# Two down projections of a decoder layer, from eight half-size block products to seven

## The chip, the cores and the metric

One core of a Trainium2 chip runs the whole program in one launch. The metric is the device time of one execution in microseconds (us); the value given is the median of three runs. The profile shows one execution, its times counted from the start of its span. In the text, PE is TensorE, DVE is VectorE, ACT is ScalarE, POOL is GpSimd and SP is the engine whose queue issues nearly all loads and stores; PSUM and SBUF are the two on-chip memories.

## The reference: what is computed

A decoder layer on 1024 tokens of width 1024: a feed-forward half step, a token mixer with two branches, and a second feed-forward half step. Cut to what matters here (the two half steps have their own weights and modulation vectors; `sh`, `sc`, `gt` are three of nine vectors that `silu(c) @ w_mod + b_mod` gives):

```python
def swiglu(h, w_gate, w_up, w_down):          # h [1024, 1024], w_gate, w_up [1024, 2816], w_down [2816, 1024]
    return (jax.nn.silu(h @ w_gate) * (h @ w_up)) @ w_down
h = rms_norm(x, g_pre_ffn1[l]) * (1 + sc1) + sh1
x = x + 0.5 * gt1 * rms_norm(swiglu(h, w_gate1[l], w_up1[l], w_down1[l]), g_post_ffn1[l])
u = rms_norm(x, g_pre_mix[l]) * (1 + sc2) + sh2
y = hybrid_mixer(u, positions, w_in[l], ...)
x = x + gt2 * rms_norm(y, g_post_mix[l])
```

All inputs and the output are fp32. The change concerns `@ w_down`, once in each half step.

## The kernel before

**Products.** Every matmul operand is a pair, hi (fp32r) and lo (the rest). `split` (L75 to L77) makes it: ACT copies the source to hi, DVE subtracts hi from the source to get lo; `psplit` (L79 to L82) has GpSimd subtract. A product is three matmuls, `mm3` (L102 to L106): hi·hi (L104), lo·hi (L105), hi·lo (L106).

**Stages.** They follow each other in the program: the first vectors of the modulation; FFN1's `gate_up`; FFN1's `down`; the mixer (`mixer_front`, `branch_b`, branch A, `mixer_out`); FFN2's `gate_up`; FFN2's `down`. All DMA loads and most stores are issued by SP, in the order of the program. The order on each engine is set by the framework's scheduler, which simulates a timeline of the program.

**gate_up** (L252 to L361) makes act = silu(h w_gate) * (h w_up), transposed, in DRAM (`actd`, 22 chunks of 128 rows by 1024 tokens). It works in 11 blocks of two chunks; each block is seven products (`i` 0 to 6) of half size, each with eight `mm3` chains into banks `gu`, 168 matmuls of 128x512 a block. GpSimd adds blocks of the raw weights `rw` (L286 to L289), `split` makes `wh` and `wl` of them three products ahead (LOOK), DVE adds the results to partial sums `p` (L343, L346), ACT takes the silu (L349), GpSimd multiplies (L351), and SP stores to `actd` (L353). In FFN1 the products 0 and 1 of the first five blocks (EARLY) come first, then products 2 to 6 of these blocks, then blocks 5 to 10 whole.

**The filler.** FFN1's `gate_up` runs a generator beside its products, `mod_rest` (L166 to L201): seven vectors of the modulation. One step (of 126) loads a [128, 512] tile `wr` of `w_mod` (four buffers, shared with a partial sum of the early blocks) and multiplies it into `macc` on DVE (L183, L185); after eight such steps `macc` is split (`mah`, `mal`), summed by PE (`mo`, L191, L192), and a row is finished on DVE (L194 to L199) and written to DRAM. Two steps (FILL) run after each product of blocks 5 to 10; the other 42 steps run in FFN1's `down`.

**down** (L368 to L425) computes G * (act w_down): three groups, columns 0 to 511 for all eight token tiles, then columns 512 to 1023 for token tiles 0 to 3, then for tiles 4 to 7. A group runs over all 22 chunks: one `mm3` per tile and chunk into bank `dn`, 1056 matmuls of 128x512 in all. The weights `rd` and the act tiles (kept in SBUF, `room`, made by `rooms`, L1158) are split for each group anew (`dh`, `dl`, `ah`, `al`). `evac` (L363 to L366) takes a bank: ACT squares it with a sum, DVE multiplies it by the gain. While the third group runs, the generator `post` works on tokens 0 to 511, one step per chunk, because their rows are complete: 

- FFN1: `post1` (L1234): `residual` (L1129, one 1024-wide DVE operation and eight or so 128x1 ones), `prenorm` (L1136, the same again), then `emit_hT` (L115), which transposes the four tiles on PE (L122) into `uh` and `ul` (L123, L124), the operand of `mixer_front`, whose first product is `cpj<-wc0h,uh`.
- FFN2: `post2` (L1337): residual and the store of the output, with the 128x1 operations on GpSimd except for the last tile.

## Time and profile before

| | us |
|---|---|
| runs | 2540.12, 2541.58, 2545.11 |
| median | 2541.58 |
| span of the profiled execution | 2537.8 |
| FFN1 gate_up: early products, blocks 0 to 4, blocks 5 to 10 | up to 119, to 263, to 498.8 |
| FFN1 down | 498.8 to 754.3 |
| mixer | 754.3 to about 2000 |
| FFN2 down, then what follows its last matmul | 2284.8 to 2525.7, to 2537.8 |
| PE busy | 2393.8 (94% of the span) |

The profiled execution is known by its span alone. The median of the runs stands 3.8 us above the span, the lowest run 2.3 us. Read it first by engine (who is busy for nearly the whole span), then by stage (the windows), then by the waits inside a stage: an engine that is idle for long in one stage may be the one that others wait for in another.

### The profile page before, as it was taken

What the parts mean: (1) busy time and instruction counts of PE and PEld (TensorE: products, weight loads), DVE (VectorE), ACT (ScalarE), POOL (GpSimd) and SP (SyncE); (2) the same over time, 40 slices, a digit from 0 to 9 for tenths busy, and PEclk for the clock granted to TensorE, in tenths of its full rate; (3) what the DMA queues carried; (4) which work ended last, traced back from release to release, by engine and by line L of the source; (5) the groups of instructions that cost most, each with busy time, mean ns of one, the idle gap of its engine ahead of it and who ended that gap; (6) DMA issues with size and microseconds to landing.
All of it is one profiled execution on the core that took longest, in us unless ns stands there. A gap on an engine that the chain in (4) does not pass through costs nothing.

```text
span 2537.8 us, 34341 instructions
## 1 busy us (share of the span) xinstructions
PE 2393.8 (94%) x11471; PEld 2017.5 (79%) x11471; DVE 1613.0 (64%) x3209; ACT 1096.6 (43%) x2358; POOL 953.3 (38%) x1109
## 2 busy tenths in 40 slices
...
GB/s 280 89 109 128 149 154 158 253 203 50 193 137 110 79 84 115 181 26 94 12 40 53 79 66 64 51 183 144 111 123 123 97 75 90 86 188 111 51 108 149
DMA packets 226222, 291.67 MB, mean 115 GB/s; under 512 B 23095, under 2 KB 145879, under 8 KB 226045
## 3 DMA queue, kind: packets, MB, share of 16 engines
...
q14 instruction: 87, 0.70, 0.1%
...
## 4 chain that ended last, share of the span: by engine, by line
PE 75%; DVE 11%; DMA 5%; issue 3%; POOL 3%; ACT 2%; SPq 0%; DVEq 0%; POOLq 0%; ACTq 0%
PE gu L105 8%; PE gu L104 8%; PE gu L106 8%; PE dn L105 6%; PE dn L106 6%; PE dn L104 6%; DMA wr<-in_w_mod_dram 3%; PE gpj L104 2%; PE gpj L105 2%; PE gpj L106 2%; PE bq L104 2%; PE bq L105 2%; PE bq L106 2%; PE bv L105 1%; PE bv L106 1%
## 5 line engine op out<-in xcount | busy, mean ns | idle before, releaser
L104 PE MATMUL gu<-V,wh 128*128 128x512 f32 x1232 | 489.6, 398 | 16.5 <-ACT wh L76 8.4
L105 PE MATMUL gu<-V,wl 128*128 128x512 f32 x1232 | 488.8, 397 | 6.8 <-DVE wl L77 6.1
L106 PE MATMUL gu<-V,wh 128*128 128x512 f32 x1232 | 483.4, 395 | 5.1 <-DVE V L77 5.1
L77 DVE TENSOR_TENSOR wl<-rw,wh 128x512 fp32r<-128x512 f32 x232 | 215.1, 930 | 136.3 <-PE gu L105 94.4
L104 PEld LDWEIGHTS gu<-V,wh 128*128 128x128 f32 x1232 | 235.7, 191 | 70.3 <-ACT wh L76 9.1
L105 PEld LDWEIGHTS gu<-V,wl 128*128 128x128 f32 x1232 | 235.3, 191 | 61.7 <-DVE wl L77 10.0
L106 PEld LDWEIGHTS gu<-V,wh 128*128 128x128 f32 x1232 | 234.0, 190 | 57.5 <-DVE V L77 7.9
L105 PE MATMUL dn<-dh,al 128*128 128x512 f32 x704 | 275.6, 392 | 1.5 <-DVE al L77 1.4
L106 PE MATMUL dn<-dl,ah 128*128 128x512 f32 x704 | 274.6, 391 | 0.0
L104 PE MATMUL dn<-dh,ah 128*128 128x512 f32 x704 | 253.7, 391 | 6.0 <-DVE junk L197 6.0
L76 ACT CAST wh<-rw 128x512 fp32r<-128x512 f32 x232 | 140.0, 618 | 208.3 <-PE gu L106 125.4
L351 POOL TENSOR_TENSOR p<-p 128x512 f32<-128x512 f32 x86 | 129.0, 1500 | 245.5 <-ACT wh L81 68.7
L343 DVE TENSOR_TENSOR p<-gu,p 128x512 f32<-128x512 f32 x252 | 170.2, 682 | 65.1 <-PE gu L106 35.1
L76 ACT CAST ah<-act 128x512 fp32r<-128x512 f32 x176 | 107.5, 621 | 182.6 <-PE dn L105 133.0
L77 DVE TENSOR_TENSOR al<-act,ah 128x512 fp32r<-128x512 f32 x176 | 118.2, 690 | 83.9 <-PE dn L105 40.8
L104 PEld LDWEIGHTS dn<-dh,ah 128*128 128x128 f32 x704 | 132.6, 189 | 33.9 <-DVE junk L197 6.4
L105 PEld LDWEIGHTS dn<-dh,al 128*128 128x128 f32 x704 | 132.8, 189 | 30.5 <-DVE al L77 3.0
L77 DVE TENSOR_TENSOR dl<-rd,dh 128x512 fp32r<-128x512 f32 x132 | 91.3, 692 | 102.1 <-PE dn L105 50.4
L106 PEld LDWEIGHTS dn<-dl,ah 128*128 128x128 f32 x704 | 132.9, 189 | 27.8
L349 ACT ACTIVATE p<-p 128x512 f32<-128x512 f32 x86 | 54.5, 633 | 215.6 <-DVE p L343 161.8
L185 DVE SCALAR_TENSOR_TENSOR macc<-wr,scol,macc 128x512 f32<-128x512 f32 x98 | 93.9, 958 | 52.2 <-DMA wr<-in_w_mod_dram 51.4
L76 ACT CAST dh<-rd 128x512 fp32r<-128x512 f32 x132 | 81.7, 619 | 84.9 <-PE dn L105 71.3
...
## 6 DMA issues: line engine op xcount, KB each, us to landing
...
```

The lines of the kernel that those rows point to most:

```text
L76: self.nc.scalar.copy(hi, src)
L77: self.nc.vector.tensor_sub(lo, src, f(hi))
L104: mm(out, ah, bh, start=start, stop=False)
L105: mm(out, al, bh, start=False, stop=False)
L106: mm(out, ah, bl, start=False, stop=stop)
L185: nc.vector.scalar_tensor_tensor(acc, r, self.scol[:, k:k + 1], acc, op0=ALU.mult, op1=ALU.add)
L343: nc.vector.tensor_tensor(x[m], bk, y[m], op=ALU.add)
L349: nc.scalar.activation(x[0], x[0], AF.Silu)
L351: nc.gpsimd.tensor_tensor(x[1], x[1], x[0], op=ALU.mult)
```

## The change

`down` becomes seven products of half size. With act^T split into four blocks (rows: halves of the 2816; columns: halves of the tokens) and w_down into four, P1 to P7 are 4 token tiles x 11 chunks x 3 matmuls each, 132, so 924 per FFN where there were 1056. Two sets of four banks take turns. The sums of act blocks are made in place by GpSimd (44 operations of 128x512 per FFN, in P2, P3 and P4); the four sums of w_down's blocks are made by the generator `mix_down`, GpSimd again, and go to a DRAM tensor `wx`: 22 tiles per FFN, each two loads of 256 KB, four subtractions of 128x256 and four stores of 128 KB, three steps a tile. For FFN1 they run as a filler in `gate_up`, one step after each product from product 2 of block 0 on, with two steps of `mod_rest` beside each (`both`); `mod_rest` now ends inside `gate_up`. For FFN2 they run in `branch_b`, five steps per token tile of its groups 1 and 2. The results are put together by `o1` to `o7`: DVE adds, ACT squares from SBUF, GpSimd multiplies by the gain in 12 of 16 cases. Tokens 0 to 511 are complete when P6 ends, so `post(0)` runs beside P7, and `post(1)` after it.

The diff, cut to its core:

```diff
-FILL = 2            # steps of the filler after each product or chunk
+FILL = 1
...
-                if filler is not None and b >= len(early):
+                if filler is not None:
...
+    def mix_down(self, pool, wd, out):
         nc = self.nc
...
+        NJ = DFF // P // 2
+        for j in range(NJ):
+            for q in range(2):
+                r = pool.tile([P, 2, 2, 256], F32, name="wx", bufs=1)
+                for e in range(2):
+                    nc.sync.dma_start(r[:, e], wd[0, (NJ * e + j) * P:(NJ * e + j + 1) * P, :]
+                                      .rearrange("p (c f) -> p c f", c=2)[:, :, q * 256:(q + 1) * 256])
+                yield
+                b11, b12, b21, b22 = (r[:, e, c] for e in range(2) for c in range(2))
+                sub = lambda o, x, y: nc.gpsimd.tensor_tensor(o, x, y, op=ALU.subtract)
+                sub(b11, b12, b11)
+                sub(b12, b22, b12)
+                sub(b22, b22, b11)
+                sub(b21, b22, b21)
+                yield
+                for n, t in enumerate((b11, b22, b12, b21)):
+                    nc.sync.dma_start(out[n, j * P:(j + 1) * P, q * 256:(q + 1) * 256], t)
+                yield
+    def down(self, W, W2, wd, wx, rooms, actd, y, G, junk, ss, post):
+        nc = self.nc
+        NJ = DFF // P // 2
+        tags = (("tr", "tr", "o", "gg"), ("pj", "pj", "s", "pt"))
+        a11, a12, a21, a22 = (rooms[n] for n in ("11", "12", "21", "22"))
+        src = lambda n, j: actd[j + NJ * (n[1] == "2"), :, 512 * (n[0] == "1"):512 * (n[0] == "1") + 512]
+        load = lambda n, j: nc.sync.dma_start(rooms[n][j], src(n, j))
+        add = lambda o, x, z, op: nc.gpsimd.tensor_tensor(o, x, z, op=op)
+        raw = lambda r, c: wd[0, r * NJ * P:(r + 1) * NJ * P, c * 512:(c + 1) * 512]
+        dsl = [slice(0, 512), slice(512, 1024)]
+        C = lambda r, c, t: y[2 - r][:, t, dsl[c - 1]]
+        sq = lambda r, c, t: ss[4 * (2 - r) + t][:, c - 1:c]
+        V = nc.vector.tensor_tensor
+        def normed(r, c, t, E):
+            nc.scalar.activation(junk(), C(r, c, t), AF.Square, accum_out=sq(r, c, t))
+            E.tensor_tensor(C(r, c, t), C(r, c, t), G[:, dsl[c - 1]], op=ALU.mult)
+        def o1(b, t):
+            nc.scalar.copy(C(2, 2, t), b)
+        def o4(b, t):
+            nc.scalar.copy(C(2, 1, t), b)
+        def o2(b, t):
+            V(C(1, 1, t), C(2, 2, t), b, op=ALU.add)
+            normed(1, 1, t, nc.gpsimd)
+        def o6(b, t):
+            V(C(1, 2, t), C(2, 2, t), b, op=ALU.add)
+            add(C(2, 1, t), C(1, 2, t), C(2, 1, t), ALU.subtract)
+        def o5(b, t):
+            V(C(1, 2, t), C(1, 2, t), b, op=ALU.add)
+        def o7(b, t):
+            for c in (1, 2):
+                V(C(2, c, t), C(2, 1, t) if c == 1 else C(1, 2, t), b, op=ALU.add)
+                normed(2, c, t, nc.gpsimd if c == 1 else nc.vector)
+        def o3(b, t):
+            V(C(1, 2, t), C(1, 2, t), b, op=ALU.add)
+            normed(1, 2, t, nc.gpsimd)
+        def s14(j):
+            load("12", j)
+            load("21", j)
+        def s1(j):
+            add(a22[j], a21[j], a22[j], ALU.add)
+        def s23(j):
+            add(a21[j], a11[j], a21[j], ALU.subtract)
+            add(a11[j], a22[j], a11[j], ALU.subtract)
+        none = lambda j: None
+        prods = [(None, raw(0, 0), 0, o1, lambda j: load("22", j), none),
+                 (a22, wx[3], 1, o4, s14, s1),
+                 (a12, raw(1, 0), 0, o2, lambda j: load("11", j), s23),
+                 (a11, wx[1], 1, o6, none, lambda j: add(a12[j], a12[j], a11[j], ALU.subtract)),
+                 (a22, wx[0], 0, o5, none, none),
+                 (a21, wx[2], 1, o7, none, none),
+                 (a12, raw(1, 1), 0, o3, none, none)]
         bg = iter(())
...
+        for n, (A, B, s, end, before, after) in enumerate(prods):
+            bk = [self.bank("dn", tag=x) for x in tags[s]]
+            final = n == len(prods) - 1
+            nlate = LATE + (W2 is not None) * 2 if final else 1
+            late = []
+            def mul(t, j, w, a):
+                ts = slice(t * P, (t + 1) * P)
+                self.mm3(bk[t], a[0][:, ts], a[1][:, ts], w[0], w[1], j == 0, j == NJ - 1)
+            for j in range(NJ):
+                before(j)
+                if j % 2 == 0:
+                    m = min(2, NJ - j)
                     r = self.raw([P, 2, 512], "rd")
...
+                    nc.sync.dma_start(r[:, 0:m], B[j * P:(j + m) * P, :].rearrange("(k p) f -> p k f", p=P))
+                    if A is None:
+                        ra = self.raw([P, 2, 512], "ra")
+                        nc.sync.dma_start(ra[:, 0:m], actd[j:j + m, :, 512:1024].rearrange("c p f -> p c f"))
+                pool = W2 if W2 is not None and final and NJ - nlate <= j < NJ - nlate + 2 else W
+                w = [pool.tile([P, 512], F32R, name=f"d{x}", tag="w") for x in "hl"]
+                self.split(w[0], w[1], r[:, j % 2])
+                a = [pool.tile([P, 512], F32R, name=f"a{x}", tag="w") for x in "hl"]
+                self.split(a[0], a[1], ra[:, j % 2] if A is None else A[j])
+                after(j)
+                if j >= NJ - nlate:
+                    late.append((j, w, a))
                     continue
...
+                for t in range(4):
+                    mul(t, j, w, a)
+                if final:
                     next(bg, None)
...
+                    next(bg, None)
             for _ in bg:
                 pass
...
+            for t in range(4):
                 for x in late:
                     mul(t, *x)
...
+                end(bk[t], t)
+            if end is o7:
+                bg = post(0)
+            if final:
+                bg = post(1)
         for _ in bg:
             pass
...
-    def branch_b(self, uT, W, bp, last, gates, raws):
+    def branch_b(self, uT, W, bp, last, gates, raws, mix):
...
+                mix = mix(self.rawp)
...
+                if g:
+                    for _ in range(5):
+                        next(mix, None)
...
+    def both(a, b):
+        while True:
+            done = True
+            for g, n in ((a, 2), (b, 1)):
+                for _ in range(n):
+                    for _ in g:
+                        done = False
+                        break
+            if done:
+                return
+            yield
...
     def rooms(fp):
-        """Room of [128, 512] for each chunk and half of the tokens: 16 of each half in big, the others in fp[half]."""
-        r = [L.big.tile([P, 8, 512], F32, name="act", tag="big") for _ in range(4)]
-        f2 = [[fp[h].tile([P, 512], F32, name=f"act{c}{h}") for h in range(2)] for c in range(16, DFF // P)]
-        return [[r[2 * h + c // 8][:, c % 8] for h in range(2)] for c in range(16)] + f2
-
-    # first half step
+        r = {}
+        for n in ("22", "21", "12", "11"):
+            t = L.big.tile([P, 8, 512], F32, name="act", tag="big")
+            r[n] = [t[:, c] for c in range(8)] + [fp[n[0] == "1"].tile([P, 512], F32, name=f"act{n}{c}") for c in range(3)]
+        return r
...
-            fill = L.mod_rest(wk, jkf)
+            wx1 = L.dram.tile([4, DFF // 2, 512], F32, name="wx1")
+            mix = L.mix_down(fs, aps["w_down1"], wx1)
+            fill = both(L.mod_rest(wk, jkf), mix)
             GU([(b, i) for b in range(EARLY) for i in range(2, 7)] + [(b, i) for b in range(EARLY, NB) for i in range(7)], fill)
+            for _ in fill:
+                pass
...
-            L.down(W, None, aps["w_down1"], room, actd, y, A1, lambda: jkb, ss, post1, fill)
-
...
+        wx2 = L.dram.tile([4, DFF // 2, 512], F32, name="wx2")
...
-            L.branch_b(uT, W, bp, lambda: L.topk(sc, ixp, mask, off, bp), lambda: L.gates(uT, gp), raws)
+            L.branch_b(uT, W, bp, lambda: L.topk(sc, ixp, mask, off, bp), lambda: L.gates(uT, gp), raws,
+                       lambda p: L.mix_down(p, aps["w_down2"], wx2))
...
-            L.down(W, W2, aps["w_down2"], room, actd, y, G3, lambda: jk, ss, post2)
+            L.down(W, W2, aps["w_down2"], wx2, room, actd, y, G3, lambda: jk, ss, post2)
```

The order of the instructions shows three places where the change moves work. The first is DVE in block 7 of FFN1's `gate_up`, from a `p_...` addition of one product to the first addition of the next (`macc` and `mal` are the filler's, `wl` the lo parts of weights, `junk` a finished row of the modulation). Before:

```order
L343 TENSOR_TENSOR p_2879<-gu,p_2879 128x512
L185 SCALAR_TENSOR_TENSOR macc<-wr,scol,macc 128x512
L77 TENSOR_TENSOR wl_3100<-rw_2815,wh_3099 128x512
L77 TENSOR_TENSOR mal<-macc,mah 128x512
L343 TENSOR_TENSOR p_2879<-gu,p_2879 128x512
L77 TENSOR_TENSOR wl_3109<-rw_2817,wh_3108 128x512
L77 TENSOR_TENSOR wl_3148<-rw_2815,wh_3147 128x512
L77 TENSOR_TENSOR wl_3152<-rw_2817,wh_3151 128x512
L343 TENSOR_TENSOR p_3172<-gu,p_3125 128x512
```

The same place with the change:

```order
L343 TENSOR_TENSOR p_3235<-gu,p_3235 128x512
L77 TENSOR_TENSOR wl_3482<-rw_3163,wh_3481 128x512
L183 TENSOR_SCALAR macc<-wr,scol 128x512
L185 SCALAR_TENSOR_TENSOR macc<-wr,scol,macc 128x512
L77 TENSOR_TENSOR wl_3525<-rw_3161,wh_3524 128x512
L185 SCALAR_TENSOR_TENSOR macc<-wr,scol,macc 128x512
L197 TENSOR_TENSOR junk_95<-mo,junk_95 1x512
L185 SCALAR_TENSOR_TENSOR macc<-wr,scol,macc 128x512 x2
L77 TENSOR_TENSOR wl_3529<-rw_3163,wh_3528 128x512
```

More of the filler stands between the same additions and splits: counted over blocks 5 to 9, 57 rows of `macc` become 95, 7 of `mal` become 12, and 14 short `junk` rows become 20, beside unchanged 70 additions and 60 `wl`.

The second place is PE at the end of FFN1's `down`, up to the first product of the mixer (`tr` are the transposes of tokens 0 to 511). Before:

```order
L104 MATMUL dn<-dh,ah 128x512
L105 MATMUL dn<-dh,al 128x512
L106 MATMUL dn<-dl,ah 128x512
L122 MATMUL tr_6202<-ident,y_4135 128x128 x4
L122 MATMUL tr_6229<-ident,y_4135 128x128 x4
L104 MATMUL cpj<-wc0h,uh_6032 128x384
```

With the change (seven more rows of `tr_6367` and `tr_6374` stand ahead of these, and the last `dn` ahead of them):

```order
L122 MATMUL tr_6374<-ident,y_4551 128x128
L122 MATMUL tr_6401<-ident,y_4551 128x128 x4
L122 MATMUL tr_6408<-ident,y_4551 128x128 x4
L122 MATMUL tr_6437<-ident,y_4551 128x128 x4
L122 MATMUL tr_6444<-ident,y_4551 128x128 x4
L122 MATMUL tr_6471<-ident,y_4551 128x128 x4
L122 MATMUL tr_6478<-ident,y_4551 128x128 x4
L104 MATMUL cpj<-wc0h,uh_6365 128x384
```

Before, six of the eight groups of transposes stand between matmuls of the last group; now all eight stand behind the last `dn`.

The third place is the end of POOL's program, in FFN2's `down` (`L411` is the gain of `normed`, the 128x1 rows are the reciprocal roots of `post2`). Before:

```order
L88 TENSOR_SCALAR rs_v<-sums 128x1
L89 TENSOR_SCALAR rs_y<-rs_v 128x1
L94 TENSOR_SCALAR rs_t<-rs_y,rs_v 128x1
L95 TENSOR_SCALAR rs_y<-rs_t,rs_y 128x1
L94 TENSOR_SCALAR rs_t<-rs_y,rs_v 128x1
```

With the change:

```order
L411 TENSOR_TENSOR y_21420<-y_21420,G_21421 128x512
L94 TENSOR_SCALAR rs_t<-rs_y,rs_v 128x1
L89 TENSOR_SCALAR rs_y<-rs_v 128x1
L94 TENSOR_SCALAR rs_t<-rs_y,rs_v 128x1
L95 TENSOR_SCALAR rs_y<-rs_t,rs_y 128x1
```

Behind the last wide operation, 19 rows of 128x1 remain (none of 128x512 stood among the last rows before, where one chain of eight was left).

## Rows read from the trace of the kernel before

**Rows 1.** The page, busy time, share of the span and instructions of each engine.
```profile
PE 2393.8 (94%) x11471; PEld 2017.5 (79%) x11471; DVE 1613.0 (64%) x3209; ACT 1096.6 (43%) x2358; POOL 953.3 (38%) x1109
```
**Rows 2.** Windows by stage; stretch, length, busy PE, PEld, DVE, ACT, POOL, PEclk, DMA share, GB/s.
```profile
263.00:498.80 235.80, 232.90 (x1005) 188.22 (x1004) 189.76 (x242) 70.50 (x128) 125.22 (x77) 1.00 0.56 174
498.80:754.30 255.50, 249.13 (x1092) 204.24 (x1092) 165.40 (x309) 106.71 (x199) 3.16 (x2) 0.99 0.46 152
2284.80:2525.70 240.90, 239.71 (x1058) 198.02 (x1056) 113.34 (x174) 95.29 (x178) 22.20 (x51) 1.00 0.30 99
500.00:520.00 20.00, 14.05 (x50) 11.03 (x49) 12.51 (x19) 5.16 (x9) 3.16 (x2) 0.83 1.03 360
```
**Rows 3.** Lines by form, DVE, 263 to 498; busy, mean ns, idle before, releasers.
```profile
L185 DVE SCALAR_TENSOR_TENSOR macc<-wr,scol,macc 128x512 f32<-128x512 f32 x58 | 61.7, 1065 | 27.2 <-DMA wr<-in_w_mod_dram 26.7
L77 DVE TENSOR_TENSOR wl<-rw,wh 128x512 fp32r<-128x512 f32 x69 | 56.7, 824 | 0.0
```
**Rows 4.** Waits, 263 to 498; us in total, times, longest.
```profile
DVE macc L185 <- DMA wr<-in_w_mod_dram: 26.7, 26, 2.4
...
PE gu L105 <- DVE wl L77: 1.9, 3, 0.9
```
**Rows 5.** Timeline, PE, inside FFN1's down (36 intervals); start, us, operation.
```profile
614.62 0.39 PE L106 MATMUL dn<-dl,ah 128*128 128x512 f32 x1
...
622.78 0.39 PE L106 MATMUL dn<-dl,ah 128*128 128x512 f32 x1
```
**Rows 6.** Waits of PE, 498.8 to 624.
```profile
PE dn L104 <- DVE junk L197: 6.0, 1, 6.0
```
**Rows 7.** Chain of waits around the start of FFN1's down; start, us, what.
```profile
498.78 5.57 DMA act<-act
...
508.42 0.43 PE dn L104
```
**Rows 8.** Timeline, PE, from the last dn of FFN1's down to the mixer.
```profile
754.33 1.03 PE L122 MATMUL tr<-ident,y 128*128 128x128 f32 x8
759.36 0.69 PE L104 MATMUL cpj<-wc0h,uh 128*128 128x384 f32 x1 [3.99 <-ACT wc0h L81]
```
**Rows 9.** Timeline, DVE, around the same place.
```profile
755.31 0.69 DVE L366 TENSOR_TENSOR y<-dn,A 128x512 f32<-128x512 f32 x1
755.92 0.15 DVE L1132 TENSOR_TENSOR sums<-sums 128x1 f32<-128x1 f32 x1
...
757.97 0.44 DVE L95 TENSOR_SCALAR rs_y<-rs_t,rs_y 128x1 f32<-128x1 f32 x3
...
758.88 0.20 DVE L95 TENSOR_SCALAR sums<-rs_t,rs_y 128x1 f32<-128x1 f32 x1
```
**Rows 10.** Lines by form, DVE, 690 to 756.
```profile
L1134 DVE SCALAR_TENSOR_TENSOR xt<-y,sums,xt 128x1024 f32<-128x1024 f32 x4 | 5.1, 1280 | 0.0
```
**Rows 11.** Lines by form, DVE, 505 to 690.
```profile
L185 DVE SCALAR_TENSOR_TENSOR macc<-wr,scol,macc 128x512 f32<-128x512 f32 x32 | 23.9, 748 | 10.1 <-DMA wr<-in_w_mod_dram 9.9
```
**Rows 12.** Timeline, POOL, in gate_up's block 5.
```profile
283.08 1.30 POOL L82 TENSOR_TENSOR wl<-s,wh 128x512 fp32r<-128x512 f32 x1
...
286.05 1.75 POOL L82 TENSOR_TENSOR wl<-s,wh 128x512 fp32r<-128x512 f32 x1
```
**Rows 13.** Timeline, DVE, the same stretch.
```profile
285.45 1.18 DVE L77 TENSOR_TENSOR wl<-rw,wh 128x512 fp32r<-128x512 f32 x1
286.56 0.68 DVE L343 TENSOR_TENSOR p<-gu,p 128x512 f32<-128x512 f32 x1
287.16 1.19 DVE L77 TENSOR_TENSOR wl<-rw,wh 128x512 fp32r<-128x512 f32 x1
```
**Rows 14.** Lines by form, POOL, 1485 to 1760, the nearest shape to the new subtractions.
```profile
L938 POOL TENSOR_TENSOR br<-br 128x256 f32<-128x256 f32 x8 | 6.2, 794 | 0.0
```
**Rows 15.** Timeline, POOL, behind the last dn of FFN2's down (at 2525.55).
```profile
2528.34 0.34 POOL L94 TENSOR_SCALAR rs_t<-rs_y,rs_v 128x1 f32<-128x1 f32 x1
2528.79 0.27 POOL L95 TENSOR_SCALAR rs_y<-rs_t,rs_y 128x1 f32<-128x1 f32 x1
```

43 lines of the change are left out of this document (1 added, 42 removed).

## The prediction

> **What bounds the kernel now.** Read first the engines' shares: PE is busy for 94% of the span, DVE for 64%, POOL for 38% [rows 1]. So PE sets the time and matmuls taken out count, as long as no other engine becomes the last one where they go or where their preparation lands. The windows say where that could be [rows 2]. In FFN2's down PE is busy for 239.7 of 240.9 us: what is saved there is saved. In FFN1's down 6 us are missing at its start (below). In blocks 5 to 10 of FFN1's gate_up PE is busy for 232.9 of 235.8 us, but DVE for 189.8 and POOL for 125.2: the stage with the least room for more vector work, and the change puts some there. The lines of DVE in that stage show which operations fill it, and that its idle time ahead of `macc` is a wait for the `wr` loads [rows 3, 4]; PE has waited for `wl` only 1.9 us [rows 4]. DVE is close behind, not yet late.
>
> **The matmuls.** 1056 become 924 in each FFN, 264 fewer in all. 36 intervals of `dn` take 8.16 us, 0.2267 us each [rows 5]: **-59.9 us**. The number of hi/lo splits stays near what it was (154 pairs per FFN), and a product's 11 chunks need two splits each per 2.72 us of matmuls, 1.4 us of DVE.
>
> **The start of FFN1's down.** The first `dn` waited 6.0 us for a `junk` row of the filler, which held its bank [rows 6], and PE then ran at the lower of its two clocks, 1.2 GHz: spacings of 0.43 us [rows 7], granted 0.83 over 20 us [rows 2]; 17% of 20 us is 3.4. With the filler done earlier this bank is free: **-9.4**. The other end is 0: the chain has the act load at 504.35, only 2 us ahead of the first `dn` [rows 7]. I take the first because the wait is put down to the `junk` row, and the act load had landed before it [rows 6, 7].
>
> **The end of FFN1's down.** Before, rows of tokens 0 to 511 were done a whole group (60 us) before the end, and `post1` and six of eight groups of transposes lay beside it; from the last transposes to the first `cpj` were 5.0 us [rows 8]. Now these rows are complete only when P6 ends, 132 x 0.2267 = 29.9 us before the end. Beside P7 stand, on DVE, 22 splits, 12 additions and gains of 128x512, 52 small operations and three of 1024 columns. Spacings are 0.61 us for a 512-wide operation and 0.15 for a small one (six from 757.97 to 758.88) [rows 9]; the 1024-wide take 1.28 [rows 10]: 34 x 0.61 + 52 x 0.15 + 3 x 1.28 = 32 us. DVE is thus full through P7. After it come, up to the last `ul`: 4 additions and 8 `ul` (7.7 us), 84 small (12.6) and 13 of 1024 columns (about 16), some 36 us, of which 4 lie beside the last tiles' matmuls and 2 behind the first `cpj`. The gap becomes about 29 us: **+24**. At least it is 12 (if DVE gets half of it done earlier, in PE's shadow), at most 36. What of `post(1)` is in it need not be done in the mixer: **-2**.
>
> **FFN1's gate_up, blocks 5 to 9.** The order puts 38 more `macc`, 5 more `mal` and 6 more short rows there. At 1065 ns, 824 ns (as `wl`) and about 1 us [rows 3] that is 40.5 + 4.1 + 6 = 51 us on DVE, whose idle time in the whole stretch is 235.8 - 189.8 = 46 us [rows 2]; 39 of it waits for `wr` (26.7 of them ahead of `macc` [rows 4], the rest ahead of its first step). A block has 168 matmuls of 235.8 / 1005 = 0.2346 us, 39.4 us. DVE's work per block becomes 14 additions x 0.68 = 9.5 [rows 13], 12 `wl` x 0.82 = 9.9, 19 `macc` x 1.065 = 20.2, 2.4 `mal` = 2.0 and 4 short rows = 4.2: 45.8 us, or 41.7 if each of the 51 begins 0.08 before the recorded end of the last, as the additions do. Taken in the middle, 44 us, it is 4.6 more than PE's, 23 in five blocks.
>
> POOL adds to it. With POOL idle a `macc` takes 748 ns [rows 11], in gate_up 1065. One stretch shows why: while POOL works without a break, at 1.30 to 1.75 us an operation, DVE completes one two-input operation every 1.71 us, each 1.18, and its additions from PSUM between them stay at 0.68 [rows 12, 13]. The new subtractions, 88 of 128x256 at about 0.8 us [rows 14], 38 us of POOL in blocks 5 to 9, make such intervals more frequent. I add 3 for that and for bubbles: **+26**. Below it is nothing, if the waits for loads simply shrink; above, +55 (both are rivals). The Trainium skill, "SBUF — State Buffer", section "Who interferes with whom", speaks against this change here: a DVE instruction with two inputs in SBUF contends with GpSimd's reads, and with one such input it does not. The trace agrees in that stretch: 0.68 for the additions from PSUM, 1.18 for `wl`. Applied to every operation of both engines the rule gives the second rival below, a sum of +22 in place of -7.
>
> **Smaller terms.** Blocks 0 to 4 get the other half of the subtractions and hardly more filler; each could hold DVE for up to a microsecond [rows 12, 13], 40 us in all, most of it in the shadow of three products of lookahead: **+2** (0 to 8). In P2 to P4 POOL does 44 additions; in P3 two per chunk, 2 x 1.71 = 3.4 us against 2.72 of matmuls, but their results are needed only from P4 on: **+5** for both FFNs (0 to 15). `branch_b` gets the other 88 subtractions and 23 MB of transfers, with POOL otherwise mostly idle: **+3** (0 to 10). At the end, 19 small POOL operations at 0.41 us [rows 15] stand behind the last gain, where eight stood, 4.5 us more, and PE's last tile is otherwise taken in the same way: **+4** (0 to 10).
>
> **Sum.** -59.9 - 9.4 + 24 - 2 + 26 + 2 + 5 + 3 + 4 = -7.3. The profiled execution spans 2537.8 us, 3.8 below the median of the runs; the change is laid on the median: 2541.6 - 7.3 = **2534**. A measurement of this kernel can tell about 0.2%, 5 us, from no change.
>
> **Rivals.**
> - *The extra filler fits into DVE's waits.* DVE's 39 us of waits for `wr` are there because loads come late, four buffers at a time; if DVE merely waits less, the +26 goes and the change gives what its matmuls promise less the gap: 2541.6 - 33.3 = **2508**. For it: the waits nearly equal the 51 us of added work. Against: they are spread in pieces of up to 2.4 us [rows 4], and more steps bring more loads, not fewer.
> - *DVE and POOL take strict turns.* This one is slower than before. If each two-input DVE operation excludes each POOL operation through blocks 5 to 9, a block costs 77 / 6 = 12.8 POOL operations [rows 2] of about 1.4 us [rows 12], 17.9; 9.4 subtractions of 0.79, 7.4; and 33.4 two-input DVE operations (12 `wl`, 19 `macc`, 2.4 `mal`) of 0.70, a little under the undisturbed `macc` [rows 11], 23.4: together 48.7 us against 39.4. That is 47 us in five blocks, and some 8 of the 39 us of waits for `wr` stay: +55 in place of +26, **2563**. It decides when POOL's idle time there, now 47% [rows 2], no longer lets DVE work undisturbed. The stretch speaks for it [rows 12, 13]; a mean `macc` of 1065 ns, with POOL busy for half of the time, speaks against it [rows 3].
> - *The first products starve.* P1 and P2 load three tiles of 256 KB per chunk each, 17.3 MB in 60 us, 288 GB/s; the fastest row shows 360 [rows 2]. If only 253 are reached, as in the busiest slices of the page, they take 68.4 us, 8.5 more in each FFN, and a lower clock behind the stalls a little more: +20, **2554**.
> - *The change does not do what it says*: the order shows 924 `dn` per FFN, so no chance.
>
> **How the numbers follow.** My forecast has 0.40: the counts are from the order and the prices from rows of the same stage. The first rival has 0.27, the second 0.23, the third 0.10. Faster by more than 5 us: all but 0.01 of the first rival, a little over half of the forecast (its own range is 2515 to 2553, by the bounds of the gap and of the smaller terms), and some of the others: 0.51. Slower by more than 5 us: nearly all of the second and most of the third rival, and 0.05 of the forecast: 0.34. Within: 0.15. The range reaches from below the first rival's time, by the 12 us by which the gap may be shorter, to above the second's by 9, for the smaller terms: **2495 to 2572**; less than 2 in 10 are outside.
>
> **What would show it.** Right: 924 `dn` per FFN at 0.227 us; FFN2's down shorter by 30 us; no wait on `junk` at the start of FFN1's down; `cpj` some 29 us after the last `dn`, ended by DVE; PE's waits for `wl` in blocks 5 to 9 grown from 1.9 to some 25 us. Wrong, for the faster side: `macc` waits for `wr` shrunk to nothing and PE without waits. For the slower side: a mean `macc` of 1.3 us and more and a `gate_up` longer by 50. The sum as a whole is wrong if POOL's additions in P2 to P4 make PE wait, which would show as `dn` waiting for `al`.

## The result: slower by 95 us, and where it went

The changed kernel takes 2636.07 us (median of 4 runs) where the kernel before takes 2540.85 (also 4): ratio 1.0378, 95% interval 1.0362 to 1.0394. The profiled execution spans 2637.4 us against 2537.8, 99.6 more. Divided at the starts of the first and last matmuls of each stage, which both profiles show (differences are taken before rounding):

| stage | before | after | difference |
|---|---|---|---|
| FFN1 gate_up, first to last `gu` | 474.0 | 546.7 | +72.8 |
| FFN1 down, first to last `dn` | 255.0 | 231.7 | -23.3 |
| last `dn` to first `cpj` | 5.3 | 38.4 | +33.1 |
| mixer, to FFN2's first `gu` | 1076.8 | 1084.3 | +7.5 |
| FFN2 gate_up | 448.6 | 448.5 | 0.0 |
| FFN2 down, first to last `dn` | 240.6 | 239.3 | -1.3 |
| behind the last `dn` | 12.3 | 22.9 | +10.6 |

The page of the changed kernel, engines, answers to [rows 1]:

```profile
PE 2383.8 (90%) x11207; PEld 1986.5 (75%) x11207; DVE 1769.9 (67%) x3233; ACT 1104.0 (42%) x2374; POOL 1301.9 (49%) x1405
```

There are 264 matmuls fewer, 59.9 us at 0.2267, but PE's busy time fell by only 10 us; its share fell from 94 to 90%. A matmul is recorded with 0.39 us and in an unbroken run one starts every 0.2267, so after each break more of it counts as busy: in the window of P3 below, 113 matmuls are busy for 28.26 us at the full clock, where 113 x 0.2267 is 25.6. Where the granted clock falls they stand further apart besides. GpSimd has 349 us more. The windows by stage, with the columns of [rows 2]:

```profile
280.00:572.00 292.00, 257.82 (x1031) 203.73 (x1030) 240.87 (x295) 76.03 (x134) 176.81 (x126) 0.93 0.70 222
572.00:803.90 231.90, 217.67 (x925) 172.71 (x923) 175.02 (x233) 100.32 (x188) 93.29 (x59) 0.99 0.38 129
803.90:842.10 38.20, 9.04 (x34) 5.60 (x32) 36.32 (x106) 14.10 (x28) 8.31 (x11) 0.56 0.50 169
2375.20:2614.60 239.40, 221.07 (x925) 174.71 (x923) 172.75 (x183) 98.45 (x188) 116.06 (x94) 0.97 0.37 123
```

In FFN1's late gate_up the granted clock is 0.93 where it was 1.00: PE stops there again and again. Not all of the 72.8 us is lost there: the 841st `gu` matmul, the first after as many as blocks 0 to 4 hold, starts 20.7 us later than before, counted from the first `gu`, and the rest adds 52.1. In both downs PE should be busy for all of 209.5 us and needs 22 to 30 more.

**The products.** 132 matmuls take 29.9 us at full pace. P1 to P7 took 38.1, 33.2, 37.4, 32.0, 29.9, 29.9 and 31.2 us in FFN1, and 38.3, 33.3, 37.4, 32.7, 29.9, 29.9 and 37.8 in FFN2, both from the starts of every 132nd `dn` in the timeline, the last up to the start of the last `dn`. Those that are not delayed, P5 and P6, are the ones with neither sums of act nor a stage border beside them.

**P1 in FFN1.** Waits between 572 and 612 us (`ra` are the act tiles of P1, `ah` their hi parts):

```profile
ACT ah L76 <- DMA ra<-act: 14.6, 3, 6.7
...
PE dn L104 <- ACT ah L76: 5.9, 2, 3.6
```

On SP's queue 14 loads of act tiles for later products stand between three loads of `ra` (issued at 563.83, 571.97 and 584.19).

**P3 in FFN1.** A window inside it, the lines by form of DVE and POOL there, and what PE waits for in it:

```profile
644.00:676.00 32.00, 28.26 (x113) 20.16 (x112) 32.00 (x20) 11.47 (x21) 32.00 (x20) 1.00 0.21 70
```
```profile
L77 DVE TENSOR_TENSOR al<-act,ah 128x512 fp32r<-128x512 f32 x10 | 17.8, 1780 | 0.0
L77 DVE TENSOR_TENSOR dl<-rd,dh 128x512 fp32r<-128x512 f32 x10 | 17.7, 1772 | 0.0
...
L402 POOL TENSOR_TENSOR act<-act 128x512 f32<-128x512 f32 x12 | 20.6, 1739 | 0.0
L402 POOL TENSOR_TENSOR act<-act,act 128x512 f32<-128x512 f32 x8 | 13.8, 1738 | 0.0
```
```profile
PE dn L105 <- DVE al L77: 3.7, 10, 0.4
```

Both engines are busy for 32.00 of 32 us, with 20 operations each (those across the edges of the window included): strictly one and one in this window, 1.7 us from start to start. DVE's splits, 0.69 us alone, are recorded at 1.78, with no idle time before them: the wait for the other engine stands inside the instruction, and the busy share hides it.

**gate_up.** What PE waits for between 230 and 572 us, and what SP waits for from 225 on:

```profile
PE mo L191 <- ACT mah L76: 41.4, 12, 11.3
PE mo L192 <- DVE mal L77: 4.1, 5, 1.3
```
```profile
SPq L387 <- POOL wx L380: 43.7, 35, 3.3
SPq L176 <- DVE macc L185: 39.0, 42, 2.0
SPq L353 <- POOL p L351: 29.4, 14, 6.2
```

PE doesn't wait for weights (`wl` 0.6 us there) but for the filler's own two matmuls, which stand in its order ahead of `gu` matmuls that could run. In PE's order the pairs `mo` stand 59 to 86 `gu` matmuls apart from block 4 into block 9, which take 13 to 20 us at 0.2267; before they stood 96 and 120 apart in turns. The filler's `macc` rows come more slowly than that: 112 of them take from 242.9 to 536.0 us, 2.6 us each, 21 us for the eight that a pair needs.

**The gap ahead of the mixer**, PE's timeline:

```profile
803.75 0.39 PE L106 MATMUL dn<-dl,ah 128*128 128x512 f32 x1
810.85 0.66 PE L122 MATMUL tr<-ident,y 128*128 128x128 f32 x2 [6.71 <-POOL band L515]
...
824.55 0.66 PE L122 MATMUL tr<-ident,y 128*128 128x128 f32 x2 [10.13 <-DVE sums L95]
...
842.12 0.69 PE L104 MATMUL cpj<-wc0h,uh 128*128 128x384 f32 x1 [4.06 <-ACT wc0h L81]
```

DVE is busy for 36.3 of these 38.2 us, with 106 operations (the third window above). The first wait bears the name of POOL's `band` because that operation ended last by the profile; the transposes read `y`, which was done on DVE at 810.7.

**The end of FFN2's down.** The waits in its last product, and the chain of waits behind the last `dn` (which starts at 2614.5; start, us, what):

```profile
DVE xt L1219 <- POOL sums L95: 6.5, 4, 4.1
...
PE dn L105 <- DVE al L77: 5.3, 1, 5.3
```
```profile
2618.80 1.27 POOL y L411
...
2624.48 0.25 POOL sums L95
...
2626.20 2.09 DMA out_dram<-xt
...
2628.35 0.73 DMA xt<-x
2629.09 3.90 issue
2632.99 0.75 DVE xt L1457
```

GpSimd's gains and 128x1 operations reach to 2624.7 in this chain, 10 us behind the last `dn`. Only then is an output stored, which frees the buffer (`xt` has three) into which the last tile's residual input is loaded, and the last operation on DVE follows that load (the profile names no releaser for the 3.90 us). This load is issued 13.8 us behind the last `dn`; before, it was 1.6.

### The profile page after: what moved, and what is told of

The parts are those of the page before. It is cut to its first block, busy times and chain, and to the rows that moved or that the text cites. A ratio compares the mean times of both kernels' runs of the same rounds, so it can differ in the third digit from the quotient of the medians.

```text
span 2637.4 us, 34776 instructions
## 1 busy us (share of the span) xinstructions
PE 2383.8 (90%) x11207; PEld 1986.5 (75%) x11207; DVE 1769.9 (67%) x3233; ACT 1104.0 (42%) x2374; POOL 1301.9 (49%) x1405
## 4 chain that ended last, share of the span: by engine, by line
PE 54%; DVE 16%; DMA 10%; issue 5%; POOL 4%; ACT 2%; SPq 0%; DVEq 0%; ACTq 0%; POOLq 0%
PE gu L106 5%; PE gu L104 5%; PE gu L105 5%; PE dn L105 4%; PE dn L106 3%; PE dn L104 3%; DMA wr<-in_w_mod_dram 3%; DVE al L77 2%; PE gpj L104 2%; DVE macc L185 2%; PE gpj L105 2%; PE gpj L106 2%; PE bq L104 2%; PE bq L106 1%; PE bq L105 1%
## 5 line engine op out<-in xcount | busy, mean ns | idle before, releaser
L105 PE MATMUL dn<-dh,al 128*128 128x512 f32 x616 | 247.3, 402 | 21.5 <-DVE al L77 21.5
L106 PE MATMUL dn<-dl,ah 128*128 128x512 f32 x616 | 242.3, 394 | 0.0
L380 POOL TENSOR_TENSOR wx<-wx 128x256 f32<-128x256 f32 x176 | 162.2, 922 | 108.9 <-DMA wx<-in_w_down_dram 85.0
L77 DVE TENSOR_TENSOR dl<-rd,dh 128x512 fp32r<-128x512 f32 x154 | 160.6, 1044 | 81.5 <-ACT dh L76 42.9
L104 PE MATMUL dn<-dh,ah 128*128 128x512 f32 x616 | 195.9, 394 | 11.1 <-ACT ah L76 11.1
L105 PEld LDWEIGHTS dn<-dh,al 128*128 128x128 f32 x616 | 117.3, 190 | 63.0 <-DVE al L77 39.3
L104 PEld LDWEIGHTS dn<-dh,ah 128*128 128x128 f32 x616 | 116.5, 190 | 37.3 <-ACT ah L76 12.7
L77 DVE TENSOR_TENSOR al<-act,ah 128x512 fp32r<-128x512 f32 x132 | 144.6, 1096 | 0.0
L402 POOL TENSOR_TENSOR act<-act 128x512 f32<-128x512 f32 x64 | 108.0, 1716 | 65.7 <-DVE al L77 65.5
L106 PEld LDWEIGHTS dn<-dl,ah 128*128 128x128 f32 x616 | 117.4, 191 | 23.5
```

What stands on the lines that cost most here:

```text
L77: self.nc.vector.tensor_sub(lo, src, f(hi))
L104: mm(out, ah, bh, start=start, stop=False)
L105: mm(out, al, bh, start=False, stop=False)
L106: mm(out, ah, bl, start=False, stop=stop)
L380: sub = lambda o, x, y: nc.gpsimd.tensor_tensor(o, x, y, op=ALU.subtract)
L402: add = lambda o, x, z, op: nc.gpsimd.tensor_tensor(o, x, z, op=op)
```

## The experiments

Each starts from the changed kernel unless it says otherwise, and each is read by its stages, since they don't touch each other. Up to the section on FFN2 alone each time is of one execution, beside 2536 to 2540 us for the kernel before.

### The sums of act on DVE

```diff
-        add = lambda o, x, z, op: nc.gpsimd.tensor_tensor(o, x, z, op=op)
+        add = lambda o, x, z, op: nc.vector.tensor_tensor(o, x, z, op=op)
```

> The changed kernel with the 44 sums of act blocks (and the one subtraction per tile of the fourth product's end) on DVE in place of GpSimd, both FFNs. Theory L (GpSimd's two-input additions and DVE's two-input operations exclude each other, 1.71 us a pair): P2, P3, P4 fall from 33.2, 37.4, 32.0 (FFN1) and 33.3, 37.4, 32.7 (FFN2) to 30, 30 to 32, 30, kernel 22 to 26 us faster, and DVE's al falls from 1.1 to about 0.7 us. Rival (these products wait for their loads): no product changes by more than 2 us.

2608.15 us. P2, P3 and P4 take 29.9 us each, in both FFNs, 12.8 and 13.6 us less in all. A window of P3, and DVE's lines in it:

```profile
635.50:665.40 29.90, 29.90 (x133) 24.77 (x132) 23.73 (x39) 13.36 (x25) 0.00 (x0) 1.00 0.31 99
```
```profile
L77 DVE TENSOR_TENSOR dl<-rd,dh 128x512 fp32r<-128x512 f32 x11 | 7.6, 690 | 6.0 <-ACT dh L76 5.9
L77 DVE TENSOR_TENSOR al<-act,ah 128x512 fp32r<-128x512 f32 x11 | 7.5, 684 | 0.0
L402 DVE TENSOR_TENSOR act<-act 128x512 f32<-128x512 f32 x7 | 4.8, 685 | 0.1
```

DVE now does all the work of two engines, and is less busy than before, 23.7 of 29.9 us: theory L holds, and the rival is out. The additions that were moved to GpSimd to spare DVE cost DVE a wait of 1.1 us each in P3, more than the 0.69 us of doing them.

### P1's act tiles

```diff
-                    if A is None:
+                    if A is None and j < 4:
...
-                self.split(a[0], a[1], ra[:, j % 2] if A is None else A[j])
+                if A is None and j >= 4:
+                    nc.sync.dma_start(a12[j], actd[j, :, 512:1024])
+                self.split(a[0], a[1], (ra[:, j % 2] if j < 4 else a12[j]) if A is None else A[j])
```

> The changed kernel with the act tiles of P1 from the fifth chunk on loaded into the tiles that later take block a12, so that the prefetch of a12 can't run ahead of them. Theory P (P1 waits for its own act tiles behind the 33 tiles of later products on the queue): P1 falls from 38.1 and 38.3 us to 31 or less, kernel 12 to 16 us faster. Rival (P1 is slow because the buffers come free only with the end of gate_up): P1 stays above 36, as the new tiles come free no earlier.

2603.26 us. P1 takes 30.0 and 29.9 us. Its windows, in the changed kernel and then here, for FFN1:

```profile
572.00:610.10 38.10, 32.15 (x133) 25.79 (x132) 15.13 (x22) 13.36 (x24) 4.10 (x3) 0.96 0.96 352
```
```profile
564.60:594.50 29.90, 29.90 (x133) 24.75 (x132) 14.97 (x22) 13.14 (x24) 4.63 (x3) 1.00 1.02 375
```

The queues are as full as before (352 and 375 GB/s) and PE never stops. So the rate was not the trouble: the loads for later products stood ahead of the ones that PE needed. Theory P holds. The time fell by more than the 16 us of the two P1: gate_up came out 7.4 us and the mixer 10.6 us shorter, in code that this edit doesn't touch; the scheduler lays out the whole program anew for each edit. (Five kernels here have the same code for gate_up and took 539.4 to 546.7 us.) A difference of up to some 10 us in a stage can have that cause, and is no evidence by itself below.

### The order of the products

```diff
-        C = lambda r, c, t: y[2 - r][:, t, dsl[c - 1]]
+        C = lambda r, c, t: y[r - 1][:, t, dsl[c - 1]]
...
+        prods = [(a11, raw(0, 0), 0, o1, lambda j: load("11", j), none),
+                 (a12, raw(1, 0), 1, o2, l2, s12),
+                 (a11, wx[1], 0, o6, none, s3),
+                 (a22, wx[0], 1, o5, none, lambda j: add(a12[j], a12[j], a11[j], ALU.subtract)),
+                 (a12, raw(1, 1), 0, o3, lambda j: load("22", j), none),
+                 (a21, wx[2], 1, o7, none, none),
+                 (a22, wx[3], 0, o4, none, none)]
...
-            if end is o7:
+            if end is o3:
                 bg = post(0)
```

> Both downs with the seven products in another order: the tokens' halves change roles, and the products are A11 B11, a12 B21, a11 wx1, a22 wx0, a12 B22, a21 wx2, a22 wx3 (a22 loaded anew), so that tokens 0 to 511 are complete after the fifth product, 60 us before the end, as they were before the change; sums of act on DVE; P1's act goes straight into its block's place; last gains on DVE; the transposes in FFN1 take banks of the other set. Nothing else differs from the changed kernel. Theory O (the 38 us gap ahead of the mixer and the 23 us tail come from the rows of tokens 0 to 511 being complete only one product before the end): gap 6 to 14 us, FFN2's last product back to 30 to 32 us and its tail to 11 to 14; each down about 212 us; kernel 65 to 85 us faster than the changed one. Rival (DVE is simply full at the end, with 28 adds where there were 16 evacuations): gap stays above 25.

The edit shown leaves out that the sums of act and the last gains move to DVE. 2572.36 us, 64 less than the changed kernel; of these 26 are the sums of act, as in the first experiment. The windows of the gap, of FFN2's down and of the tail:

```profile
801.40:809.60 8.20, 2.56 (x18) 1.76 (x16) 8.20 (x35) 4.45 (x10) 2.07 (x5) 0.88 0.33 106
2340.30:2555.40 215.10, 210.54 (x924) 172.86 (x923) 152.83 (x227) 96.69 (x183) 45.14 (x61) 1.00 0.42 137
2555.40:2570.50 15.10, 0.41 (x2) 0.00 (x0) 8.32 (x20) 0.72 (x2) 6.16 (x14) 0.61 0.48 174
```

The gap is 8.2 us with 35 operations of DVE in it, not 106; FFN2's last product is back at 29.8, its tail at 15.1: theory O holds (one microsecond over the bound for the tail). With the sums on DVE alone, in the first experiment, the gap was 38.5, FFN2's last product 38.7 and the tail 23, so the engine of the sums is not the reason; the moved gains were not tested by themselves. The sixth product, which `post(0)` now runs beside, is 2.2 and 2.6 us longer, and FFN1's seventh 2.4: the order is worth about 39 us in all. FFN2's down as a whole loses 25.5 us against before. FFN1's took 230.1, not the 212 expected, for its P1 got worse, 44.8 us. In it (POOL's row, then SP's, DVE's and PE's waits between 566 and 616 us):

```profile
584.23 17.18 POOL L351 TENSOR_TENSOR p<-p 128x512 f32<-128x512 f32 x1 [8.00 <-DVE p L343]
```
```profile
SPq L353 <- POOL p L351: 17.2, 2, 12.9
```
```profile
DVE act L402 <- DMA act<-act: 12.3, 2, 6.5
...
PE dn L105 <- DVE al L77: 9.2, 3, 3.6
```

DVE runs the sums for the second product between P1's splits, from 584.5 to 599.6 without a break. GpSimd's last multiplication of gate_up, 1.3 us by the median of its line in the changed kernel, stands for 17.18 us beside them; SP waits for it with its store, and the loads behind it on the queue come late.

### gate_up: the sums of w_down1, the filler, and each alone

Gate_up took 474.0 us before and 546.7 with the change. The first pair takes one of the two fillers away or puts it back.

```diff
-            fill = both(L.mod_rest(wk, jkf), mix)
+            fill = both(L.mod_rest(wk, jkf), iter(()))
```

> The changed kernel without the sums of w_down1's blocks: FFN1's gate_up keeps two filler steps of the modulation per product from block 0 on, FFN1's down reads plain blocks of w_down1 in the place of the four sums (so the first half step's output is left out as the reference has it). Theory Q (the sums' loads and stores stand on SP's queue between the wr loads, wait there for GpSimd, and its operations take turns with DVE's, so macc comes late and PE waits at mo): gate_up's 546.9 us (25.0 to 571.9) fall to 480 to 490, kernel some 60 us faster. Theory R (126 filler steps in blocks 4 to 9 are too many for DVE and four wr buffers, whatever stands beside them): gate_up stays above 530.

2602.27 us, gate_up 510.1: between the two theories, 36.1 over before.

```diff
-            for g, n in ((a, 2), (b, 1)):
+            for g, n in ((a, 0 if s <= 5 * EARLY else 2), (b, 1)):
...
+                if filler is not None and n in (4, 5):
+                    self.mo = "s" if n == 4 else "gg"
+                    for _ in range(7 - n):
+                        next(filler, None)
```

> The changed kernel with the modulation's filler where it was before: two steps per product of blocks 5 to 10 only, the other 42 steps in P5 and P6 of FFN1's down; the sums of w_down1 stay one step per product from block 0 on. Theory R: gate_up falls from 546.9 to within 15 of before's 474.0, PE's wait at mo under 8 us, kernel 55 to 70 us faster. Theory Q: gate_up still 510 or more. Both: P5 and P6 stay within 3 us of 29.9.

2627.38 us, gate_up 517.3: over the 510 of theory Q, but 29 less than with both. The whole filler costs 36 us without the sums, the sums cost 43 beside the filler at its old pace, and both together 73. In this run PE waits for `wl` (15.4 us) and GpSimd's `wl` (6.9), not for `mo`. P5 and P6 took 32.5 and 33.7 us, P6 a little over the bound. The kernel gained only 9 us, since FFN1's down grew to 255.0: the filler's last 42 steps stand in it again, and its first `dn` waits 5.7 us for a `junk` row, as before the change.

The sums were then taken apart, on the kernel with the filler at its old pace:

```diff
-                for n, t in enumerate((b11, b22, b12, b21)):
+                for n, t in enumerate((b11, b22, b12, b21) if xfer else ()):
```

> As that run with SP issuing, but only the 88 subtractions of w_down1's sums remain, on one tile loaded once; the other loads and all stores are left out (FFN1's down reads plain blocks in their place). Rival L: gate_up keeps most of its 43 us, 500 or more. Theory Q or traffic: it falls to 485 or less.

```diff
+                if subs:
                     sub(b11, b12, b11)
```

> The opposite: all loads and stores of w_down1's sums remain, the 88 subtractions are left out, so that plain blocks are stored. Traffic, or SP's queue: gate_up 500 or more. Rival L: 485 or less.

Gate_up took 494.8 us with the subtractions alone (+21) and 504.7 with the transfers alone (+31). The transfers are over the bound of their theory, the subtractions between the two; the parts come to 51, 8 more than both at once (43). Of the 31 us of the transfers 21 are lost by the 841st `gu`, where the kernel with both parts has lost 8, so the parts are not simply added. Two attempts to make the sums cheap failed:

```diff
-                    nc.sync.dma_start(out[n, j * P:(j + 1) * P, q * 256:(q + 1) * 256], t)
+                    (nc.gpsimd if own else nc.sync).dma_start(out[n, j * P:(j + 1) * P, q * 256:(q + 1) * 256], t)
```

> As the run with the modulation's filler where it was before (gate_up 517.3 us, 43 more than before the change), but the loads and stores of w_down1's sums are issued by GpSimd, which makes the sums, so that SP's queue no longer waits for it. Theory Q (43 us of waits of SP for GpSimd's sums hold back the loads of weights and wr behind them): gate_up at 490 or less. Rival L (GpSimd's sums themselves take turns with DVE): 510 or more.

2696.99 us: gate_up 531.5, and P2 of FFN1's down stood 66 us over its 29.9 for the sums, which came too late. SP was rid of the wait for the sums and nothing was gained; what makes the transfers cost 31 us stays open.

```diff
-            for g, n in ((a, 0 if s <= 5 * EARLY else 2), (b, 1)):
+            for g, n in ((a, 0 if s <= 5 * EARLY else 2), (b, 3)):
...
-                sub = lambda o, x, y: nc.gpsimd.tensor_tensor(o, x, y, op=ALU.subtract)
+                sub = lambda o, x, y: (nc.vector if W2 else nc.gpsimd).tensor_tensor(o, x, y, op=ALU.subtract)
```

> As the run with the modulation's filler where it was before, but the sums of w_down1's blocks are made by DVE, three steps per product of blocks 0 to 4, so that they are done or nearly done before the filler begins. If the two fillers only disturb each other and what stands beside GpSimd: gate_up near 480, at most 490 (517.3 with GpSimd and one step per product). Rival (the sums' transfers through one buffer are too slow for the early blocks and go on behind them, on the same queue): 500 or more.

2634.86 us, gate_up 527.7: the rival. The sums went on to 385 us, far behind the early blocks. By the 841st `gu` it was already 27 us behind (285.7 against 258.2), and PE waited 27.8 us for DVE's additions `p` in the whole of gate_up. What DVE does for nothing in the down, where it has room, it can't do in the early blocks.

### gate_up: what makes the filler dear

These four stand on the run without the sums (gate_up 510.1, +36).

```diff
-                    r = pool.tile([P, 512], F32, name="wr", tag="wr", bufs=4)
+                    r = (more.tile([P, 512], F32, name="wr2", bufs=2) if k % 2 else
+                         pool.tile([P, 512], F32, name="wr", tag="wr", bufs=4))
```

> As the run without the sums of w_down1's blocks, but every other wr tile comes from two buffers of their own, six in all, which neither px nor the split of macc takes. Theory B (the filler's chain of load, macc, free buffer, next load is what is late: in that run it stretched gate_up to 510 us with PE waiting 21 us at mo): gate_up falls by 15 us or more, PE's wait at mo under 10. Rival D (DVE has too many two-input operations beside GpSimd's): less than 6 us change.

2594.72 us, gate_up 506.3: 3.8 us less, the rival's side; more buffers alone aren't it.

```diff
-                        nc.vector.scalar_tensor_tensor(acc, r, self.scol[:, k:k + 1], acc, op0=ALU.mult, op1=ALU.add)
+                        nc.vector.tensor_scalar(acc, r, self.scol[:, k:k + 1], None, op0=ALU.mult)
```

> As the run without the sums of w_down1's blocks (gate_up 510.1, 36 more than before the change), but macc keeps no sum: each step is a multiplication with one input in SBUF, as the first of eight is (so the modulation's seven vectors are left out as the reference has them). All loads and buffers stay. If DVE's two-input operations beside GpSimd are the cost: gate_up 485 or less. If the loads and the filler's chain are: 500 or more.

```diff
-                    r = pool.tile([P, 512], F32, name="wr", tag="wr", bufs=4)
-                    nc.sync.dma_start(r, i["w_mod"][0, k * P:(k + 1) * P, c0:c0 + 512])
+                    if k == 0:
+                        r = pool.tile([P, 512], F32, name="wr", tag="wr", bufs=4)
+                        nc.sync.dma_start(r, i["w_mod"][0, k * P:(k + 1) * P, c0:c0 + 512])
```

> As that run with the full macc, but the seven steps after the first use the first one's tile: 14 loads in place of 112 (the seven vectors are left out as the reference has them). If DVE's two-input operations are the cost: gate_up 500 or more; if the loads are: 485 or less. If both runs lie between, each takes a part.

2594.32 and 2595.25 us, gate_up 501.6 and 500.0: without the second input, and without seven of eight loads, 8.5 and 10.2 of the 36 us go, not clear of what the layout alone can do. Neither run reached the bound of 485. In both PE still waits at `mo`, 16.3 and 12.7 us.

```diff
+                    if k == 4 and pend:
+                        pend()
...
-                ah = pool.tile([P, 512], F32R, name="mah", tag="wr", bufs=4)
-                al = pool.tile([P, 512], F32R, name="mal", tag="wr", bufs=4)
+                ah = more.tile([P, 512], F32R, name="mah", bufs=1)
+                al = more.tile([P, 512], F32R, name="mal", bufs=1)
...
-                nc.tensor.matmul(b, self.ones, ah, start=True, stop=False)
-                nc.tensor.matmul(b, self.ones, al, start=False, stop=True)
+                pend = finish
```

> As the run without the sums of w_down1's blocks (gate_up 510.1 us, PE waits 21 us at mo), but the split of macc has two tiles of its own and the two matmuls mo, with the row behind them, are emitted four steps later. If their place in PE's order is what costs: PE's wait at mo under 5 us, gate_up 490 or less. If the filler's DVE work holds up the weights and additions themselves: the waits move to wl and p, gate_up stays above 500.

2572.90 us. The wait at `mo` and the stretch of gate_up, in the run without the sums (first) and with `mo` later:

```profile
PE mo L191 <- ACT mah L76: 21.2, 11, 4.5
```
```profile
PE mo L197 <- ACT mah L76: 11.7, 8, 3.0
```
```profile
225.00:534.50 309.50, 284.69 (x1177) 224.83 (x1176) 255.04 (x331) 84.57 (x150) 148.33 (x90) 0.97 0.59 185
```
```profile
225.00:514.70 289.70, 276.97 (x1177) 222.59 (x1176) 262.65 (x331) 84.96 (x150) 152.28 (x90) 0.99 0.65 205
```

With the same loads, the same operations on DVE and GpSimd and the same matmuls, gate_up takes 490.2 us, 20 of the 36 us less. The edit also leaves the four `wr` buffers to the loads; two more buffers alone were worth 3.8 us above, so most of the 20 is the place of `mo` in PE's order. By the two windows PE's idle time fell by 12.1 us, and its busy time for the same 1177 matmuls by 7.7, with the granted clock back from 0.97 to 0.99. The wait at `mo` is still 11.7 us, not under the 5 expected. The 16 us that remain are shared by the rest of the wait and by DVE; how, no run shows. Nor was the later `mo` tried together with the sums.

### The mixer

```diff
-                if g:
-                    for _ in range(5):
-                        next(mix, None)
```

> The changed kernel without the sums of w_down2's blocks (FFN2's down reads plain blocks in their place, so the second half step's product is left out as the reference has it). It prices these sums where they are made, in branch_b: the mixer took 1084.3 us from cpj to FFN2's gate_up against 1076.7 before. If the sums cost that, it falls to 1077, kernel 7 to 8 us faster; if the mixer's start (the second half of the tokens, postponed) is the cause, it stays above 1082.

2619.23 us, the mixer 1070.4 against 1084.3. That is more than the sums were expected to cost, but the run with P1's loads, which keeps them, also came to 1073.7. With FFN2 alone (below) the mixer stands at 1084.1 with the sums in it, behind an unchanged gap of 5 us, and at 1082.8 in the kernel that has them elsewhere, behind a gap of 2.0. So the mixer moves by this much without the sums too, and their price there is not shown.

### Seven products in FFN2 alone

Three kernels leave FFN1 as it was before the change, so that the filler and gate_up are untouched, and use the other order with the sums of act on DVE in FFN2.

```diff
-            L.down(W, None, aps["w_down1"], wx1, room, actd, y, A1, lambda: jkb, ss, post1)
+            L.down8(W, None, aps["w_down1"], room, actd, y, A1, lambda: jkb, ss, post1, fill, mix2)
```

> Seven products in FFN2's down alone, in the order that completes tokens 0 to 511 after the fifth, sums of act on DVE, the first four chunks of P1 from tiles of their own; the sums of w_down2's blocks made by GpSimd in FFN1's down (three steps per chunk of its first group), where it was idle; FFN1 otherwise as before the change. FFN2's down 240.6 to 211 us, its tail 12 to 15, FFN1's down and the mixer as before within 5: 2510 to 2520, 20 to 30 faster than before. Rival (FFN1's down is bound by its transfers at its start, or its DVE is slowed by GpSimd): FFN1's down 10 or more longer, 2525 or more.

2575.46 us (4 runs), ratio 1.0153 (1.0136 to 1.0169): longer, clear of noise. FFN1's down grew from 255.0 to 306.2 us. The waits of PE and DVE in it:

```profile
PE dn L105 <- DVE al L77: 42.5, 9, 22.5
```
```profile
DVE macc L183 <- DMA wr<-in_w_mod_dram: 33.6, 4, 27.0
DVE macc L185 <- DMA wr<-in_w_mod_dram: 33.2, 12, 9.7
```

GpSimd being idle was no free place for the sums; the rival was right, and by more than it said. Of its two causes it was the transfers in the main: SP waited 62.1 us for the sums with their stores, the filler's `wr` loads came late behind these and held up DVE ahead of `al`, while DVE's splits grew only from 0.69 to 0.78 us.

```diff
-        prods = [(a11, raw(0, 0), 0, o1, lambda j: load("11", j), none),
+        prods = [(a12, raw(0, 0), 0, o1, none, none),
```

> FFN1 as before the change; FFN2's down with seven products in the order that completes tokens 0 to 511 after the fifth, sums of act on DVE, P1's act through tiles of their own and the places of a12; the sums of w_down2's blocks in branch_b as in the change. FFN2's down 240.6 to 211 to 215, tail 12 to 15, mixer up to 8 longer: 2517 to 2527 where before is 2540, faster by 0.4 to 0.9%. Rival (the sums cost the mixer what m1_no_mix2 showed, 14 us, and the tail 3): 2530 to 2536.

With the sums in branch_b and P1's act through other places (the edit shown is against the kernel with the other order): 2530.19 us (6 runs, 2524.75 to 2532.88), ratio 0.9955 (0.9941 to 0.9968). P1 took 40.2 us. As in P1 of the other order above, DVE's sums for the second product held GpSimd's last multiplication, here for 7.54 us, and SP behind it; `rd` came late on that queue:

```profile
SPq L353 <- POOL p L351: 9.6, 2, 7.1
```
```profile
ACT dh L76 <- DMA rd<-in_w_down_dram: 12.8, 1, 12.8
...
PE dn L104 <- ACT ah L76: 5.4, 1, 5.4
```

```diff
-        prods = [(a12, raw(0, 0), 0, o1, none, none),
+        prods = [(a11, raw(0, 0), 0, o1, lambda j: load("11", j), none),
```

> As b5_ffn2_only, but P1's act goes straight into the place of a11. P1 33 to 34 us in place of 40.2, FFN2's down 215 in place of 222, kernel 2521 to 2526, 0.5 to 0.8% faster than before the change. Rival (P1's length hangs on what the scheduler puts on DVE around it): P1 stays near 40.

P1 took 34.2 us. 2522.31 us (5 runs, before 2539.35 in 9), ratio 0.9937, 95% interval 0.9923 to 0.9950: faster than both kernels, by 0.6%. Its windows of the mixer, FFN2's down and the tail:

```profile
757.20:1841.30 1084.10, 1020.84 (x5490) 897.15 (x5491) 696.59 (x1854) 565.71 (x1414) 448.23 (x680) 0.97 0.35 109
2289.20:2505.50 216.30, 210.95 (x925) 172.76 (x923) 154.12 (x229) 96.71 (x183) 45.77 (x61) 1.00 0.41 136
2505.50:2520.50 15.00, 0.15 (x1) 0.00 (x0) 8.05 (x20) 0.72 (x2) 5.85 (x14) 0.68 0.48 175
```

Of the 29.9 us that the matmuls of one FFN are worth, 24.5 arrive in the down; the mixer takes back 7.3 and the tail 3.0. That leaves 14.2 of the 17.3 us between the two profiles; the other 3 lie in stages that this kernel leaves as they were.

## Why the prediction was wrong

The forecast was 2534 us, no difference that matters, in a range up to 2572; measured are 2636. The largest step that failed is the one for FFN1's gate_up, which set DVE's work in a block against PE's; others failed beside it. Point by point:

- **The matmuls, -59.9**: right, 1848 `dn` at 0.2267 us. P5 and P6 show it. But FFN2's down is not 30 us shorter, it is 1.3: the products beside them gave the rest back.
- **The start of FFN1's down, -9.4**: wrong in kind. The wait on `junk` went, as said, but P1 waited for its own act tiles: 38.1 us where the first 132 `dn` of before took 38.9. FFN2, where nothing had been counted, lost 8.4 there too. The third rival had the place and nearly the size (+20 against 8.2 + 8.4), and its cause only half: the order on the queue, not its rate.
- **P2 to P4, +5 for both FFNs**: measured 12.8 and 13.6. The price was right, 3.4 us per chunk in P3 (37.4 measured, 11 x 3.42 = 37.6), and the step "their results are needed only from P4 on" failed. The results were not late; the splits on DVE were, because the turns are taken by both engines, and PE waited for `al`, which the prediction had named as the sign that its sum is wrong. The Trainium skill ("SBUF — State Buffer", section "Who interferes with whom") says that a DVE instruction with two inputs in SBUF contends with a GpSimd instruction that reads SBUF. The trace agrees: 20 operations of each in 32.00 us, the splits at 1.78 where they take 0.69 with GpSimd idle.
- **The end of FFN1's down, +24**: the mechanism was right, the size was 33. DVE is busy for 36.3 us in the gap, the whole of the sum of 36, from which 6 had been taken off as lying beside the last matmuls and behind the first `cpj`. Some 2.9 of the 36.3 are new: beside GpSimd's last gains two `sums` of 128x1 took over 1 us where others take 0.14, and a `y` 2.3 where others take 1.28.
- **gate_up, +26 for blocks 5 to 9 and +2 for blocks 0 to 4**: measured 52 and 21, 73 in all. The second rival had the size of the first with its 55, but not the mechanism: its sign, a mean `macc` of 1.3 us and more, did not come (1073 ns against 1065). I asked how much DVE has to do, and read the slack from `wl`, for which PE hardly waits even now (0.6 us, not the 25 forecast). What I left out is that the filler ends in two matmuls on PE, which stand in a fixed order: a filler that is late stops PE itself, 45.5 us here, and the granted clock falls to 0.93. In the kernel without the sums `mo` later gave back 20 of 36 us, where taking away loads or inputs gave 10 or less. What the sums add beside the filler, 37 us, was not taken apart further than above; that part of the cause stays open.
- **FFN2's last product**, 37.8 us, was in no term: a residual on DVE waited there for GpSimd's small operations (6.5 us), and the split that PE needed stood behind it (5.3). It went with the other order.
- **The tail, +4**: +10.6. The 19 small operations were counted; the three gains of 1.3 us each that stand among small ones behind the last `dn` were not, and that the last tile's input then waits for a buffer which only an output store frees was not seen.
- **The mixer, +1 in all**: +7.5; how much of it the sums cost is not shown.

The range failed as a whole because the losses were taken as alternatives, each with its chance, where they are in different stages and came together: gate_up, P1, P2 to P4, the gap, FFN2's last product and the tail all did. Added up at their upper ends (0 for the -9.4, a gap of 36, +55, the upper ends of the smaller terms and the +20) they come to 2629 us, 7 short of the time measured.
